# Hi and lo parts of the activations side by side: one 512-column matmul for the hi weights, sums added at eviction

## The chip, the cores and the metric

The kernel runs on one core of a Trainium2 chip. The metric is device microseconds of one execution; before the change the median of three runs is 1461.11 us.

## What is computed

Two layers of a decoder trunk on x of 256 tokens by 1,024 features, all in float32. Cut to what matters:

```python
for l in range(2):
    x = x + 0.5 * swiglu(rmsnorm(x, ffn1_norm[l]), ffn1_w_in[l], ffn1_w_out[l])
    h = rmsnorm(x, mix_norm[l])
    hq, hf, hi, hg, aq, ak, av, ga, gb = split(h @ w_in[l])
    A = hgrn2_recurrence(silu(hq), 1 - f, hi, log(f)); f = lb + (1 - lb) * sigmoid(hf)
    A = rms(A) * out_norm[l] * silu(hg)
    B = three groups of dilated window attention over aq, ak, av, merged
    x = x + (sigmoid(ga) * (A @ w_a[l]) + sigmoid(gb) * (B @ w_b[l])) @ w_out[l]
    x = x + 0.5 * swiglu(rmsnorm(x, ffn2_norm[l]), ffn2_w_in[l], ffn2_w_out[l])
# swiglu(h, w1, w2): a, b = split(h @ w1); (silu(a) * b) @ w2, inner width 2816
```

## The kernel before

**Three products for one.** TensorE multiplies in float32r, a shorter form of float32. To keep the precision, each operand is split into a hi part (rounded to float32r) and a lo part (the rest), and a product is the sum of three: hi weights with hi activations, hi weights with lo activations, lo weights with hi activations.

**Weights.** `unit` loads up to eight row tiles of 128 rows by 256 columns into a buffer `raw` (three of them). In chunks of four row tiles ScalarE copies them into `whi` (L195) and VectorE subtracts to give `wlo` (L196). There are four buffers of each, so two units of weights are held at a time.

**Two forms of product.** `mm_feat` (L209 to L211) keeps a 128 by 128 piece of weights in the array and streams 256 tokens of activations: the output has features in partitions and both blocks of 128 features (`fb`) lie side by side in one PSUM bank of 512 float32 columns. For each row tile and block it issues a triple: hi weights with `ah`, hi weights with `al`, lo weights with `ah`, all three added into the same 256 columns. `full` is `unit` and `mm_feat` over 1,024 rows: 48 matmuls. `wide` with `mm_half` (L219 to L221) does it the other way round: 128 tokens stay in the array and 512 weight columns stream, two banks for the two halves of the tokens. It serves where tokens are wanted in partitions (v, g, q, k, and the last product of the kernel).

**Activations.** `xh` and `xl` are the parts of the normed input (gains go in ahead of the product, and 1/rms comes in behind it through `Rb`, one factor per token, or `rstd`). `hh` and `hl` are the parts of the ffn's inner values, `oah` and `oal` (tile names `ph`, `pl`) those of the recurrence's output, `mgh` and `mgl` (the same tiles) those of the merged branches, `obh` and `obl` those of the attention's output. Each of these is a tile of its own: [128, k, 256].

**PSUM.** Eight banks: four (`MM`) in the pool `mm` for these products, one a `full`, two a `wide`; three `sm` and one `tr` for the small ones.

**Evictions.** A `full` is evicted by one VectorE instruction that reads the bank and multiplies by `Rb` (L307, L311, L352, L362, L660) or by another operand (L675, L684), or adds to `xT` (L342, L699).

**Stages of a layer.** `ffn` (22 units in, then three units for each of four output blocks), `mix` with the recurrence (`hgrn_pair`, four times), the gates A, the attention, the products with `w_a`, gates B mixed with `branch_b` (units of half the length), the product with `w_out`, then the second `ffn`. Behind each stage's start `norm_scale` makes `Rb` from the sum of squares, while the first units of the stage are already multiplied.

**Order.** Each engine runs its queue in order. The program is written stage by stage, but the framework lays out each engine's instructions itself with a simulated timeline (`schedule_with_timeline_sim`), so small products, evictions and splits of later units are mixed, and two units can be open at the same time. A tile of a pool that is used again waits until its last reader is done.

Of the kernel before, what the change touches and what calls it, by code (L numbers as in the profile page):

```python
# [37 lines left out]
# columns of the constant table  # L38
# [9 lines left out]
def _shape_constants():  # L48
    """Identity, rotary tables and 0/1 or additive masks: functions of the shapes alone."""
# [26 lines left out]
def trunk(ctx, tc, x, ffn1_norm, ffn1_w_in, ffn1_w_out, mix_norm, w_in, lb_logits, out_norm,  # L76
# [6 lines left out]
    ps_mm = ctx.enter_context(tc.tile_pool(name="ps_mm", bufs=MM, space=PSUM))  # L83
# [81 lines left out]
    def lower_bounds():  # L165
        """Lower bounds of the decay of layer 1: softmax over depth, cumulated, less the first."""
# [16 lines left out]
    def unit(w, r0, nk, col, step=0):  # L183
# [6 lines left out]
        for a in range(0, nk, step or KH):  # L190
            n = min(step or KH, nk - a)
            hi = wts.tile([128, KH, CU], F32R, name="whi", bufs=WB)
            lo = wts.tile([128, KH, CU], F32R, name="wlo", bufs=WB)
            r = raw[:, a:a + n, :]
            nc.scalar.activation(hi[:, :n, :], r, AF.Copy)  # L195
            nc.vector.tensor_sub(lo[:, :n, :], r, hi[:, :n, :].bitcast(F32))  # L196
            parts += [(hi[:, k, :], lo[:, k, :]) for k in range(n)]
        return parts

    def mm_feat(ps, wu, ah, al, k0, nk, first, last):  # L200
        """ps[feature, fb, token] += W^T a"""
        for k in range(nk):
            hi, lo = wu[k]
            for fb in range(2):
                o = ps[:, fb * T:(fb + 1) * T]
                f = slice(fb * 128, (fb + 1) * 128)
                s = first and k == 0 and fb == 0
                e = last and k == nk - 1
                nc.tensor.matmul(o, hi[:, f], ah[:, k0 + k, :], start=s, stop=False, skip_group_check=True)  # L209
                nc.tensor.matmul(o, hi[:, f], al[:, k0 + k, :], start=False, stop=False, skip_group_check=True)  # L210
                nc.tensor.matmul(o, lo[:, f], ah[:, k0 + k, :], start=False, stop=e, skip_group_check=True)  # L211

    def mm_half(o, h, wu, ah, al, k0, nk, first, last):
        """o[token of half h, column] += a^T W"""
# [8 lines left out]
    def full(w, col, ah, al, nk=KD, step=0):  # L223
        wu = unit(w, 0, nk, col, step)
        ps = ps_mm.tile([128, 512], F32, name="mm")
        mm_feat(ps, wu, ah, al, 0, nk, True, True)
        return ps

    def wide(w, col, ah, al, nk=KD):
# [18 lines left out]
    def v2(a):  # L248
        return a.rearrange("p (a b) -> p a b", a=2)

# [41 lines left out]
    def ffn(l, gi, w1, w2, to_out, x0=None):  # L292
        norm_parts(gi, l)
        with ExitStack() as es:
            fp = es.enter_context(tc.tile_pool(name="ffn", bufs=2))
            hh = fp.tile([128, KF, T], F32R, name="hh", bufs=1)
            hl = fp.tile([128, KF, T], F32R, name="hl", bufs=1)
            xt = None
            for j in range(DFF // CU):
                pa = full(w1, j * CU, xh, xl, step=0 if j or l or gi else FIRST)  # L300
# [6 lines left out]
                nc.vector.tensor_mul(a, v2(pa), Rb2)  # L307
                nc.scalar.activation(a, a, AF.Silu)
                pb = full(w1, DFF + j * CU, xh, xl)
                b = fp.tile([128, 2, T], F32, name="fb")  # L310
                nc.vector.tensor_mul(b, v2(pb), Rb2)  # L311
# [13 lines left out]
            if to_out:  # L325
                for c in range(D // CW):
                    ps = wide(w2, c * CW, hh, hl, KF)
# [5 lines left out]
            else:  # L333
                for c in range(D // CU):
                    ps = ps_mm.tile([128, 512], F32, name="mm")
                    k0 = 0
                    for nk in (8, 8, 6):
                        wu = unit(w2, k0 * 128, nk, c * CU)
                        mm_feat(ps, wu, hh, hl, k0, nk, k0 == 0, k0 + nk == KF)
                        k0 += nk  # L340
                    xs = xT[:, 2 * c:2 * c + 2, :]
                    nc.vector.scalar_tensor_tensor(xs, v2(ps), 0.5, xs, op0=OP.mult, op1=OP.add)  # L342

# [1 line left out]
    def hgrn_pair(wp, st, l, u, pf, vg):  # L345
        W, X, ATs = st
        w = w_in[l]
        if pf is None:
            pf = full(w, MIX_HF + u * CU, xh, xl)
        f = wp.tile([128, 2, T], F32, name="hf", bufs=2)  # L350
        k = wp.tile([128, 2, T], F32, name="hk", bufs=2)
        nc.vector.tensor_mul(f, v2(pf), Rb2)  # L352
# [6 lines left out]
        pq = full(w, MIX_HQ + u * CU, xh, xl)  # L359
        z = wp.tile([128, 2, T], F32, name="hz", bufs=1)  # L360
        sg = wp.tile([128, 2, T], F32, name="hs", bufs=1)
        nc.vector.tensor_mul(z, v2(pq), Rb2)  # L362
# [5 lines left out]
        if u % 2 == 0:  # L368
            pv = wide(w, MIX_HI + u * CU, xh, xl)
# [17 lines left out]
        def suffix(B, m, kin, name):  # L387
            """products behind each m-block inside its 4m-block, and the keys carried to its end"""
# [13 lines left out]
        def diag(Y, s0, m, dst):  # L402
            """queries decayed to the start of their 4m-block: slot j for the m-block j"""
# [48 lines left out]
        def carry(m, B, last=False):  # L452
            """queries and keys from blocks of m to blocks of 2m"""
# [37 lines left out]
        if u % 2:  # L491
            pg = wide(w, MIX_HG + (u - 1) * CU, xh, xl)
# [40 lines left out]
    def attn(ap, l, obh, obl):  # L533
# [5 lines left out]
        def qk_unit(i, base, dst, g):  # L539
# [6 lines left out]
            ps = wide(w, base + g * CW, xh, xl)  # L546
# [30 lines left out]
        def v_unit(g):  # L577
            ps = wide(w, MIX_AV + g * CW, xh, xl)
# [54 lines left out]
    def mix(l):  # L633
        norm_parts(1, l)
        with ExitStack() as es:
            mp = es.enter_context(tc.tile_pool(name="mix", bufs=1))
            pf0 = full(w_in[l], MIX_HF, xh, xl)
# [20 lines left out]
            def gate(base, u, dst):  # L658
                ps = full(w, base + u * CU, xh, xl)
                nc.vector.tensor_mul(dst, v2(ps), Rb2)  # L660
# [4 lines left out]
            with ExitStack() as e2:  # L665
                ap = e2.enter_context(tc.tile_pool(name="attn", bufs=1))
                obh = ap.tile([128, 4, T], F32R, name="obh")
                obl = ap.tile([128, 4, T], F32R, name="obl")
                attn(ap, l, obh, obl)
                if l == 0:  # L670
                    lower_bounds()
                for u in range(D // CU):
                    ps = full(w_a[l], u * CU, oah, oal)
                    s = slice(2 * u, 2 * u + 2)
                    nc.vector.tensor_mul(mg[:, s, :], mg[:, s, :], v2(ps))  # L675
                mgh = mp.tile([128, KD, T], F32R, name="ph", tag="ph", bufs=1)
                mgl = mp.tile([128, KD, T], F32R, name="pl", tag="pl", bufs=1)
                gb = {}

                def branch_b(u):  # L680
                    ps = full(w_b[l], u * CU, obh, obl, nk=4)
# [14 lines left out]
            for u in range(D // CU):  # L696
                ps = full(w_out[l], u * CU, mgh, mgl)
                xs = xT[:, 2 * u:2 * u + 2, :]
                nc.vector.tensor_add(xs, xs, v2(ps))  # L699
# [31 lines left out]
```

## Time and profile before

| | before |
|---|---|
| median of three runs | 1461.11 us (1460.61 to 1461.12) |
| span of the profiled execution | 1458.1 us |
| HBM read over the span | 250.39 MB, 172 GB/s |
| weight splits, ScalarE (L195, L241) | 367.9 + 132.6 us |
| weight splits, VectorE (L196, L242) | 424.2 + 155.2 us |
| matmuls and weight loads | 11,362 each |

The profile is of one execution. Its span runs from the first to the last instruction and is 3.0 us shorter than the median of the runs. PE is TensorE's matmuls, PEld its weight loads, DVE is VectorE, ACT is ScalarE, POOL is GpSimd. L209 is line 209 of the kernel. `mm<-xh,whi` means that tile `mm` is written from `xh` and `whi`. In a view of groups, "x1920 | 540.7, 282 | 1.4" are the count, the busy time in us, the mean of one in ns and the idle time before them. Matmuls overlap in the pipeline, so their busy times add up to more than the time that passes.

### The profile page before, as it was taken

How to read it: one execution, taken by the hardware profiler on the slowest of the kernel's cores; microseconds unless marked ns; L12 is line 12 of the kernel's file. 1: busy time of each engine (PE TensorE's matmuls, PEld its weight loads, DVE VectorE, ACT ScalarE, POOL GpSimd, SP SyncE). 2: the span in 40 equal slices, each digit the busy share in tenths (PEclk: the TensorE clock that was granted, in tenths of full speed). 3: DMA queues.
4: the chain of work that ended last, by engine and by line, in shares of the span. 5: the costliest groups of instructions: out<-in, count | busy, mean ns of one | idle time of the engine just before them, and what ended most of it. 6: DMA issues, size and time to landing. Idle time of an engine off the chain costs nothing.

```text
span 1458.1 us, 26998 instructions
## 1 busy us (share of the span) xinstructions
PE 1448.9 (99%) x11362; PEld 1366.3 (94%) x11362; DVE 996.0 (68%) x1452; ACT 791.1 (54%) x1259; POOL 91.3 (6%) x86
## 2 busy tenths in 40 slices
PE   8999999999999999999999999999999999999999
PEld 8999998898889999999999999988988899999987
DVE  6666559776976586665566655698779766766653
ACT  6544447667864555444444444566577646554432
POOL 0000010002510000000000000100034000000000
PEclk9999999999999999999999999999999999999999
DMA  9565564345554365555555555544454534555552
GB/s 309 176 195 177 178 203 156 135 145 174 173 174 146 115 202 176 196 178 186 190 174 190 186 164 189 197 147 144 149 173 171 179 125 138 195 186 191 174 187 101
DMA packets 215881, 253.17 MB, mean 174 GB/s; under 512 B 4224, under 2 KB 182608, under 8 KB 215760
## 3 DMA queue, kind: packets, MB, share of 16 engines
q1 hardware_dynamic: 215584, 251.38, 51.8%
q8 instruction: 89, 1.46, 0.4%
q14 instruction: 32, 0.26, 0.1%
q10 hardware_dynamic: 176, 0.07, 0.0%
HBM read 250.39 MB, written 1.05 MB: 172 GB/s over the span
## 4 chain that ended last, share of the span: by engine, by line
PE 99%; DMA 0%; ACT 0%; SPq 0%; DVE 0%; issue 0%; ACTq 0%
PE mm L209 23%; PE mm L211 23%; PE mm L210 23%; PE mm L221 8%; PE mm L219 8%; PE mm L220 8%; PE sm L415 1%; PE sm L595 1%; PE tr L574 1%; PE sm L614 1%; PE sm L606 1%; PE sm L616 0%; DMA x<-in_x_dram 0%; PE sm L480 0%; PE sm L525 0%; PE sm L506 0%
## 5 line engine op out<-in xcount | busy, mean ns | idle before, releaser
L195 ACT ACTIVATE whi<-raw 128x1024 fp32r<-128x1024 f32 (+1 forms) x354 | 367.9, 1041 | 435.4 <-PE mm L210 339.8
L196 DVE TENSOR_TENSOR wlo<-raw,whi 128x1024 fp32r<-128x1024 f32 (+1 forms) x354 | 424.2, 1199 | 244.3 <-ACT whi L195 242.6
L209 PE MATMUL mm<-xh,whi 128*128 128x256 f32 x1920 | 540.7, 282 | 1.4 <-ACT whi L195 1.4
L211 PE MATMUL mm<-xh,wlo 128*128 128x256 f32 x1920 | 540.9, 282 | 0.0
L210 PE MATMUL mm<-xl,whi 128*128 128x256 f32 x1920 | 539.4, 281 | 0.0
L209 PEld LDWEIGHTS mm<-xh,whi 128*128 128x128 f32 x1920 | 362.6, 189 | 2.8 <-ACT whi L195 1.8
L211 PEld LDWEIGHTS mm<-xh,wlo 128*128 128x128 f32 x1920 | 362.5, 189 | 1.2 <-issue 0.4
L210 PEld LDWEIGHTS mm<-xl,whi 128*128 128x128 f32 x1920 | 362.4, 189 | 0.6
L242 DVE TENSOR_TENSOR wlo<-raw,whi 128x1024 fp32r<-128x1024 f32 x126 | 155.2, 1233 | 62.5 <-ACT whi L241 62.2
L241 ACT ACTIVATE whi<-raw 128x1024 fp32r<-128x1024 f32 x126 | 132.6, 1060 | 98.0 <-PE mm L221 53.1
L219 PE MATMUL mm<-whi,xh 128*128 128x512 f32 x416 | 166.7, 401 | 0.0
L221 PE MATMUL mm<-whi,xl 128*128 128x512 f32 x416 | 165.8, 399 | 0.0
L220 PE MATMUL mm<-wlo,xh 128*128 128x512 f32 x416 | 164.8, 396 | 0.0
L211 PE MATMUL mm<-hh,wlo 128*128 128x256 f32 x528 | 149.5, 283 | 0.0
L210 PE MATMUL mm<-hl,whi 128*128 128x256 f32 x528 | 149.5, 283 | 0.0
L209 PE MATMUL mm<-hh,whi 128*128 128x256 f32 x528 | 149.4, 283 | 0.0
L210 PEld LDWEIGHTS mm<-hl,whi 128*128 128x128 f32 x528 | 100.8, 191 | 0.0
L211 PEld LDWEIGHTS mm<-hh,wlo 128*128 128x128 f32 x528 | 100.8, 191 | 0.0
L209 PEld LDWEIGHTS mm<-hh,whi 128*128 128x128 f32 x528 | 100.8, 191 | 0.0
L221 PEld LDWEIGHTS mm<-whi,xl 128*128 128x128 f32 x416 | 78.1, 188 | 18.4
L220 PEld LDWEIGHTS mm<-wlo,xh 128*128 128x128 f32 x416 | 78.2, 188 | 17.7
L219 PEld LDWEIGHTS mm<-whi,xh 128*128 128x128 f32 x416 | 78.2, 188 | 16.9
(194 smaller groups left out, 1753.2 us busy)
## 6 DMA issues: line engine op xcount, KB each, us to landing
raw<-in_ffn_w_in_dram SPq DMA_DIRECT2D x87, 1024.0 KB, 5.1
raw<-in_w_in_dram SPq DMA_DIRECT2D x84, 1024.0 KB, 4.9
raw<-in_ffn_w_out_dram SPq DMA_DIRECT2D x34, 1024.0 KB, 5.1
raw<-in_ffn_w_out_dram SPq DMA_DIRECT2D x12, 768.0 KB, 4.4
raw<-in_w_branch_a_dram SPq DMA_DIRECT2D x8, 1024.0 KB, 5.1
raw<-in_w_out_dram SPq DMA_DIRECT2D x8, 1024.0 KB, 5.4
raw<-in_w_branch_b_dram SPq DMA_DIRECT2D x8, 512.0 KB, 3.4
x<-in_x_dram SPq DMA_DIRECT2D x4, 256.0 KB, 4.0
```

The source lines that it names most:

```text
L195: nc.scalar.activation(hi[:, :n, :], r, AF.Copy)
L196: nc.vector.tensor_sub(lo[:, :n, :], r, hi[:, :n, :].bitcast(F32))
L209: nc.tensor.matmul(o, hi[:, f], ah[:, k0 + k, :], start=s, stop=False, skip_group_check=True)
L210: nc.tensor.matmul(o, hi[:, f], al[:, k0 + k, :], start=False, stop=False, skip_group_check=True)
L211: nc.tensor.matmul(o, lo[:, f], ah[:, k0 + k, :], start=False, stop=e, skip_group_check=True)
L219: nc.tensor.matmul(o, ah[:, k0 + k, t], hi, start=s, stop=False, skip_group_check=True)
L220: nc.tensor.matmul(o, ah[:, k0 + k, t], lo, start=False, stop=False, skip_group_check=True)
L221: nc.tensor.matmul(o, al[:, k0 + k, t], hi, start=False, stop=e, skip_group_check=True)
L241: nc.scalar.activation(hi, r, AF.Copy)
L242: nc.vector.tensor_sub(lo, r, hi.bitcast(F32))
L415: nc.tensor.matmul(p[32 * b:32 * b + 32, c * n:(c + 1) * n], kk[:, o], mov(o), start=True, stop=True, tile_position=(0, 32 * b))
L574: nc.tensor.transpose(pt[:, h, c * 128:(c + 1) * 128], z[:, c, 2 * a + h, :], ident)
```

## The change

The two parts of every activation go into one tile, side by side for each row tile: `xp` is [128, k, 2, 256], with `xh` and `xl` as views of it, and `hp`, `oap`, `mgp` and `obp` likewise. In `mm_feat` the hi weights are loaded once and stream both parts as 512 columns into a whole bank, so the products with hi and with lo activations lie in its two halves; the lo weights stream the hi part into the second half. Each block of 128 features has a bank of its own, so a unit takes two banks, and the pool has two tiles of two banks in place of four of one. The sum of the halves is made at eviction: `total` copies the second halves with ScalarE and adds the first halves with VectorE, and what multiplied from PSUM then multiplies in SBUF. Where the result is added to `xT`, two VectorE instructions add the halves one after the other. Some tiles get 32 more columns, and their data starts a few columns later. Comments are dropped.

```diff
-    ps_mm = ctx.enter_context(tc.tile_pool(name="ps_mm", bufs=MM, space=PSUM))
+    ps_mm = ctx.enter_context(tc.tile_pool(name="ps_mm", bufs=MM // 2, space=PSUM))
...
+    def parts_of(pool, n, name, at, tag=None):
+        t = pool.tile([128, n * 2 * T + 32], F32R, name=name, tag=tag or name, bufs=1)
+        return t[:, at // 4:at // 4 + n * 2 * T].rearrange("p (k a t) -> p k a t", a=2, t=T)
...
-    xh = const.tile([128, KD, T], F32R, name="xh")
-    xl = const.tile([128, KD, T], F32R, name="xl")
+    xp = const.tile([128, KD, 2, T], F32R, name="xp")
+    xh, xl = xp[:, :, 0, :], xp[:, :, 1, :]
...
-            hi = wts.tile([128, KH, CU], F32R, name="whi", bufs=WB)
-            lo = wts.tile([128, KH, CU], F32R, name="wlo", bufs=WB)
+            hi, lo = (wts.tile([128, KH * CU + 32], F32R, name=x, bufs=WB)[:, 0:KH * CU].rearrange(
+                "p (k c) -> p k c", c=CU) for x in ("whi", "wlo"))
...
-                o = ps[:, fb * T:(fb + 1) * T]
                 f = slice(fb * 128, (fb + 1) * 128)
-                s = first and k == 0 and fb == 0
                 e = last and k == nk - 1
-                nc.tensor.matmul(o, hi[:, f], ah[:, k0 + k, :], start=s, stop=False, skip_group_check=True)
-                nc.tensor.matmul(o, hi[:, f], al[:, k0 + k, :], start=False, stop=False, skip_group_check=True)
-                nc.tensor.matmul(o, lo[:, f], ah[:, k0 + k, :], start=False, stop=e, skip_group_check=True)
+                nc.tensor.matmul(ps[:, fb, :], hi[:, f], ap[:, k0 + k].rearrange("p a t -> p (a t)"),
+                                 start=first and k == 0, stop=False, skip_group_check=True)
+                nc.tensor.matmul(ps[:, fb, T:2 * T], lo[:, f], ap[:, k0 + k, 0, :], start=False, stop=e,
+                                 skip_group_check=True)
...
+    def banks():
+        return ps_mm.tile([128, 2, 512], F32, name="mm")
...
+    def total(dst, ps):
+        nc.scalar.activation(dst, ps[:, :, T:2 * T], AF.Copy)
+        nc.vector.tensor_add(dst, ps[:, :, 0:T], dst)
...
     def wide(...)
-        ps = [ps_mm.tile([128, 512], F32, name="mm") for _ in range(2)]
+        pt = banks()
+        ps = [pt[:, h, :] for h in range(2)]
...
-                hi = wts.tile([128, KH, CU], F32R, name="whi", bufs=WB).rearrange("p (k a) c -> p k (a c)", a=2)
-                lo = wts.tile([128, KH, CU], F32R, name="wlo", bufs=WB).rearrange("p (k a) c -> p k (a c)", a=2)
+                hi, lo = (wts.tile([128, KH * CU + 32], F32R, name=x, bufs=WB)[:, 8:8 + KH * CU].rearrange(
+                    "p (k c) -> p k c", c=CW) for x in ("whi", "wlo"))
...
     def ffn(...)
-            hh = fp.tile([128, KF, T], F32R, name="hh", bufs=1)
-            hl = fp.tile([128, KF, T], F32R, name="hl", bufs=1)
+            hp = parts_of(fp, KF, "hp", 64)
+            hh, hl = hp[:, :, 0, :], hp[:, :, 1, :]
...
-                nc.vector.tensor_mul(a, v2(pa), Rb2)
+                total(a, pa)
+                nc.vector.tensor_mul(a, a, Rb2)
...
-                    nc.vector.scalar_tensor_tensor(xs, v2(ps), 0.5, xs, op0=OP.mult, op1=OP.add)
+                    for a in range(2):
+                        nc.vector.scalar_tensor_tensor(xs, ps[:, :, a * T:(a + 1) * T], 0.5, xs,
+                                                       op0=OP.mult, op1=OP.add)
...
     def hgrn_pair(...)
-        nc.vector.tensor_mul(f, v2(pf), Rb2)
+        total(f, pf)
+        nc.vector.tensor_mul(f, f, Rb2)
...
     def mix(l)
-            oah = mp.tile([128, KD, T], F32R, name="ph", tag="ph", bufs=1)
-            oal = mp.tile([128, KD, T], F32R, name="pl", tag="pl", bufs=1)
+            oap = parts_of(mp, KD, "pp", 96)
+            oah, oal = oap[:, :, 0, :], oap[:, :, 1, :]
+            et = mp.tile([128, 2, T], F32, name="et", bufs=1)
...
-                obh = ap.tile([128, 4, T], F32R, name="obh")
-                obl = ap.tile([128, 4, T], F32R, name="obl")
+                obp = parts_of(ap, 4, "obp", 0)
...
-                    nc.vector.tensor_mul(mg[:, s, :], mg[:, s, :], v2(ps))
+                    total(et, ps)
+                    nc.vector.tensor_mul(mg[:, s, :], mg[:, s, :], et)
...
                 def branch_b(u)
-                    nc.vector.tensor_mul(g, g, v2(ps))
+                    total(et, ps)
+                    nc.vector.tensor_mul(g, g, et)
...
-                nc.vector.tensor_add(xs, xs, v2(ps))
+                for a in range(2):
+                    nc.vector.tensor_add(xs, xs, ps[:, :, a * T:(a + 1) * T])
```

The other units (`pb`, `pq`, the gates) change as `pa` and `pf` do.

More of the change, by code (lines that the diff above doesn't have):

```diff
@@ L198, in unit, with mm_feat @@
         return parts
-    def mm_feat(ps, wu, ah, al, k0, nk, first, last):
+    def mm_feat(ps, wu, ap, k0, nk, first, last):
         for k in range(nk):
@@ L221, in mm_half, with full, wide @@
             nc.tensor.matmul(o, al[:, k0 + k, t], hi, start=False, stop=e, skip_group_check=True)
-    def full(w, col, ah, al, nk=KD, step=0):
+    def banks():
+        return ps_mm.tile([128, 2, 512], F32, name="mm")
+    def full(w, col, ap, nk=KD, step=0):
         wu = unit(w, 0, nk, col, step)
-        ps = ps_mm.tile([128, 512], F32, name="mm")
-        mm_feat(ps, wu, ah, al, 0, nk, True, True)
-        return ps
-    def wide(w, col, ah, al, nk=KD):
-        ps = [ps_mm.tile([128, 512], F32, name="mm") for _ in range(2)]
+        ps = banks()
+        mm_feat(ps, wu, ap, 0, nk, True, True)
+        return ps
+    def total(dst, ps):
+        nc.scalar.activation(dst, ps[:, :, T:2 * T], AF.Copy)
+        nc.vector.tensor_add(dst, ps[:, :, 0:T], dst)
+    def wide(w, col, ap, nk=KD):
+        pt = banks()
+        ps = [pt[:, h, :] for h in range(2)]
+        ah, al = ap[:, :, 0, :], ap[:, :, 1, :]
         for k0 in range(0, nk, 4):
@@ L306, in ffn @@
                 a = fp.tile([128, 2, T], F32, name="fa")
-                nc.vector.tensor_mul(a, v2(pa), Rb2)
+                total(a, pa)
+                nc.vector.tensor_mul(a, a, Rb2)
                 nc.scalar.activation(a, a, AF.Silu)
-                pb = full(w1, DFF + j * CU, xh, xl)
+                pb = full(w1, DFF + j * CU, xp)
                 b = fp.tile([128, 2, T], F32, name="fb")
-                nc.vector.tensor_mul(b, v2(pb), Rb2)
+                total(b, pb)
+                nc.vector.tensor_mul(b, b, Rb2)
                 nc.vector.tensor_mul(a, a, b)
@@ L326, in ffn @@
                 for c in range(D // CW):
-                    ps = wide(w2, c * CW, hh, hl, KF)
+                    ps = wide(w2, c * CW, hp, KF)
                     for h in range(2):
@@ L334, in ffn @@
                 for c in range(D // CU):
-                    ps = ps_mm.tile([128, 512], F32, name="mm")
+                    ps = banks()
                     k0 = 0
@@ L358, in hgrn_pair @@
         nc.scalar.activation(k, f, AF.Copy, scale=-1.0, bias=1.0)
-        pq = full(w, MIX_HQ + u * CU, xh, xl)
+        pq = full(w, MIX_HQ + u * CU, xp)
         z = wp.tile([128, 2, T], F32, name="hz", bufs=1)
         sg = wp.tile([128, 2, T], F32, name="hs", bufs=1)
-        nc.vector.tensor_mul(z, v2(pq), Rb2)
+        total(z, pq)
+        nc.vector.tensor_mul(z, z, Rb2)
         nc.scalar.activation(sg, z, AF.Sigmoid)
@@ L368, in hgrn_pair @@
         if u % 2 == 0:
-            pv = wide(w, MIX_HI + u * CU, xh, xl)
+            pv = wide(w, MIX_HI + u * CU, xp)
             vg["v"] = wp.tile([128, 2, CW], F32, name="hv", bufs=1)
@@ L491, in hgrn_pair @@
         if u % 2:
-            pg = wide(w, MIX_HG + (u - 1) * CU, xh, xl)
+            pg = wide(w, MIX_HG + (u - 1) * CU, xp)
             vg["g"] = wp.tile([128, 2, CW], F32, name="hgs", bufs=1)
@@ L545, in qk_unit @@
             nc.gpsimd.tensor_mul(gs[:, :, 64:128], sin_t[:, :, 64:128], gr[:, None, 0:64].to_broadcast([128, 2, 64]))
-            ps = wide(w, base + g * CW, xh, xl)
+            ps = wide(w, base + g * CW, xp)
             z = ap.tile([128, 2, 4, 128], F32, name="az", bufs=2)
@@ L577, in v_unit @@
         def v_unit(g):
-            ps = wide(w, MIX_AV + g * CW, xh, xl)
+            ps = wide(w, MIX_AV + g * CW, xp)
             for c in range(2):
@@ L658, in gate @@
             def gate(base, u, dst):
-                ps = full(w, base + u * CU, xh, xl)
-                nc.vector.tensor_mul(dst, v2(ps), Rb2)
+                ps = full(w, base + u * CU, xp)
+                total(dst, ps)
+                nc.vector.tensor_mul(dst, dst, Rb2)
                 nc.scalar.activation(dst, dst, AF.Sigmoid)
@@ L666, in mix @@
                 ap = e2.enter_context(tc.tile_pool(name="attn", bufs=1))
-                obh = ap.tile([128, 4, T], F32R, name="obh")
-                obl = ap.tile([128, 4, T], F32R, name="obl")
-                attn(ap, l, obh, obl)
+                obp = parts_of(ap, 4, "obp", 0)
+                attn(ap, l, obp[:, :, 0, :], obp[:, :, 1, :])
                 if l == 0:
```

18 lines of the change are left out of this document (9 added, 9 removed).

## The prediction

> **What bounds the kernel now.** I read the page's busy times first, then the clock, then the chain that ended last.
>
> ```profile
> span 1458.1 us, 26998 instructions
> PE 1448.9 (99%) x11362; PEld 1366.3 (94%) x11362; DVE 996.0 (68%) x1452; ACT 791.1 (54%) x1259; POOL 91.3 (6%) x86
> ...
> PEclk9999999999999999999999999999999999999999
> ...
> PE 99%; DMA 0%; ACT 0%; SPq 0%; DVE 0%; issue 0%; ACTq 0%
> ```
>
> TensorE works in 99% of the span at a granted clock of 0.9 or more in every slice, and 99% of the chain lies on it. VectorE and ScalarE have 32% and 46% of the span free. So the time is the sum of the distances from one matmul's start to the next (the pitch), and other work counts only where it makes TensorE wait. A busy record (282 ns for 256 columns) overlaps the next one and is no price; the pitch is. I take it from the view of one source line over a stretch without other matmuls: count, first start, last start.
>
> ```profile
> L209 PE MATMUL mm<-xh,whi x285: 277/280/387, 29.7 to 129.8; 128*128 128x256 f32 x143
> L209 PE MATMUL mm<-xh,whi x293: 277/281/285, 555.8 to 660.0; 128*128 128x256 f32 x147
> L209 PE MATMUL mm<-hh,whi x173: 277/283/283, 136.8 to 198.8; 128*128 128x256 f32 x173
> L209 PE MATMUL mm<-ph,whi x56: 283/283/283, 521.0 to 540.8; 128*128 128x256 f32 x56
> L219 PE MATMUL mm<-whi,xh x33: 392/399/399, 338.1 to 360.5; 128*128 128x512 f32 x33
> L219 PE MATMUL mm<-whi,hh x79: 389/389/397, 1396.0 to 1449.5; 128*128 128x512 f32 x79
> ```
>
> L209 runs once in a triple (L209, L210, L211). A triple of 256 columns takes 100.1/284 = 352.5 ns and 104.2/292 = 356.8 ns on xh, 62.0/172 = 360.5 on hh, 19.8/55 = 360.0 on ph: 117.5 to 120.2 ns a matmul. In `wide`, L219 to L221 take 22.4/32 = 700 ns with xh and 53.5/78 = 686 with hh: 233.3 and 228.6 ns for 512 columns. So 512 columns cost 1.90 to 1.99 times what 256 cost. The whole change lives in that gap.
>
> **The matmuls.** How many triples there are, by the grouped view:
>
> ```profile
> L209 PE MATMUL mm<-xh,whi 128*128 128x256 f32 x1920 | 540.7, 282 | 1.4 <-ACT whi L195 1.4
> L209 PE MATMUL mm<-hh,whi 128*128 128x256 f32 x528 | 149.4, 283 | 0.0
> L209 PE MATMUL mm<-ph,whi 128*128 128x256 f32 x256 | 71.6, 283 | 0.0
> L209 PE MATMUL mm<-obh,whi 128*128 128x256 f32 x64 | 18.2, 285 | 0.0
> L219 PE MATMUL mm<-whi,xh 128*128 128x512 f32 x416 | 166.7, 401 | 0.0
> L219 PE MATMUL mm<-whi,hh 128*128 128x512 f32 x88 | 34.3, 390 | 0.0
> ```
>
> Each of the 2,768 triples becomes a pair: one matmul of 512 columns with the hi weights, one of 256 with the lo weights. Streamed columns stay at 768; one matmul and one weight load go. Triples now: 1,920 x 354.7 (mean of the two xh rows) + 528 x 360.5 + 320 x 360.0 = 986.5 us, 356.4 each. After: no row shows the pair alternating. I take 512 at 228.6 and 256 at 356.4/3 = 118.8, so 347.4 a pair, 961.6 us: **24.9 us less**. Ends by rows: 228.6 + 117.5 = 346.1 saves 28.5 us; 233.3 + 120.2 = 353.5 saves 8.0. A loss is excluded, since even this dearest pair is below the mean triple. Far below lies the score product, which streams 256 float32 columns of both parts in 1.30/6 = 216.7 ns:
>
> ```profile
> 442.52 1.30 PE sm L595 x6
> ```
>
> A pair at 216.7 + 117.5 = 334.2 would save 61.4 us. I stay with 228.6 because it is the row with the same type, columns and weight loads.
>
> A rule speaks against the change: the Trainium skill, page "TensorE: Matmul & The Clock Gate", section "Back-to-back issue gap", gives 262 cycles at 2.4 GHz for 256 columns and 518 for 512. By it (an estimate) a triple is 327.5 ns and a pair 325.0, so the edit would save 6.9 us instead of 24.9. The trace disagrees in size: 117.5 to 120.2 and 228.6 to 233.3 ns stand against the rule's 109.2 and 215.8.
>
> **The wide matmuls** keep shape and count but their operands move. In the program before, xh starts at byte 24,704 of a partition, whi at 83,168, hh at 124,128: remainders by 128 of 0, 96 and 96. The faster wide row has equal remainders (whi with hh), the slower one unequal. The diff starts `wide`'s weights 32 bytes later, so they meet xp at 0 and 0 and hp (64 bytes later) at 0 and 32. If that is what parts the rows, 3 x 416 matmuls gain 4.7 ns and 3 x 88 lose it: **4.7 us less**. Two rows are thin ground; the ends are 0 and 5.9, and I take 4.7.
>
> **The evictions.** `total` adds, for 136 units, a ScalarE copy of 512 elements from PSUM and a VectorE add; the 20 units that end in xT get a second VectorE instruction. Nearest rows:
>
> ```profile
> L307 DVE TENSOR_TENSOR fa<-mm,Rb 128x512 f32<-128x512 f32 x44 | 30.4, 691 | 21.1 <-PE mm L211 21.0
> L580 ACT ACTIVATE av<-mm,rstd 128x512 f32<-128x512 f32 x12 | 8.2, 685 | 10.2 <-PE mm L221 10.2
> L342 DVE SCALAR_TENSOR_TENSOR xT<-mm,xT 128x512 f32<-128x512 f32 x12 | 8.2, 684 | 0.0
> ```
>
> ScalarE gets 136 x 0.685 = 93 us (884 of some 1,440), VectorE 156 x 0.69 = 108 (1,104). Neither becomes the bound; the copies lie under matmuls. What can show is latency. The add waits for the copy, with the splits (wlo) of the next units queued behind it on VectorE, and TensorE waits for those. And a unit now holds two banks: with four banks, unit n+2 may start only when unit n is evicted (before: unit n+4). In the ffn a unit lasts 16 x 347.4 = 5.6 us and its eviction some 0.7 + 0.7 plus up to one queued split of 1.2, so nothing shows. Three places are tighter:
>
> ```profile
> 200.00:260.00 60.00, 60.00 (x595) 53.81 (x594) 50.57 (x98) 39.44 (x63) 5.62 (x5) 1.00 0.52 174
> 510.00:530.00 20.00, 20.00 (x169) 20.00 (x168) 17.30 (x21) 10.22 (x13) 0.00 (x0) 1.00 0.64 211
> 1453.14 0.69 DVE L330 SCALAR_TENSOR_TENSOR fy<-mm,xt 128x512 f32<-128x512 f32 x1 [7.20 <-PE mm L221]
> 1454.49 0.69 DVE L330 SCALAR_TENSOR_TENSOR fy<-mm,xt 128x512 f32<-128x512 f32 x1 [0.67 <-PE mm L221]
> ```
>
> Columns after the stretch: PE, PEld, DVE, ACT busy. In the first pairs of `hgrn_pair` VectorE works 50.6 of 60 us and gets 4 adds (2.8); in `branch_b` 17.3 of 20 and gets 5 (3.5), while units of 24 matmuls become 2.8 us long and turn banks over twice as fast. I put 2 us to each, twice (two layers), and 1 us to stage borders and to the end, where both halves of the last product now share one tile (an eviction of 0.69 us may move behind the last matmul): **9 us more**, between 2 (all hidden) and 40 (the slower rival below).
>
> **The sum**, against the profiled execution: 1458.1 - 24.9 - 4.7 + 9 = 1437.5. Its span is 3.0 us below the median of the runs, 1461.1; with that, **1440.5 us**.
>
> **Rivals.**
>
> *The excess goes by columns, not by matmuls* (0.20). For: on xh, 233.3 is nearly 2 x 117.5. Against: on hh, 228.6 against 240.4. Then a pair is 353.5 and the wide rows stay: 1461.1 - 8.0 + 9 = 1462, spread 1455 to 1468. This is the side on which the skill's rule for the back-to-back gap falls, too.
>
> *Slower: half the banks stall TensorE at each norm* (0.13). The first units behind a norm are evicted late today, because the eviction multiplies by Rb:
>
> ```profile
> 211.92 0.40 PE L219 MATMUL mm<-whi,xh 128*128 128x512 f32 x1
> ...
> 218.24 0.69 DVE L352 TENSOR_TENSOR hf<-mm,Rb 128x512 f32<-128x512 f32 x1
> ...
> 552.32 1.23 DVE L196 TENSOR_TENSOR wlo<-raw,whi 128x1024 fp32r<-128x1024 f32 x1 [2.72 <-ACT whi L195]
> ...
> 555.79 0.28 PE L209 MATMUL mm<-xh,whi 128*128 128x256 f32 x1
> ...
> 558.56 0.69 DVE L307 TENSOR_TENSOR fa<-mm,Rb 128x512 f32<-128x512 f32 x1
> ```
>
> The third unit starts at 211.92 and the first is free at 218.93: 7.0 us short in each of two mixers. In three ffns it is 559.25 - 555.79 = 3.5. Together 24.4 us, and 5 x 1.38 for the longer eviction: 31, and with the other 9 some 40, against 29.6 gained: 1471. It decides if the add stands behind the copy into Rb on VectorE, as the code's order has it. Against it: the new pair of instructions doesn't read Rb, VectorE is idle for 2.72 us ahead of 552.32 when the first unit is done, and its order there (splits between the norm's steps) is already not the code's.
>
> *Much faster: the weight load paces the short matmuls, and a 512-column stream runs free* (0.12). A pair at 334.2 gives 1461.1 - 61.4 + 9 = 1409. Against: both wide rows have one load to 512 columns and still take 228.6 or more. By the skill's same page, section "LDWEIGHTS (loading the stationary operand)", 128 columns take 106.7 ns, as long as 256 columns take to stream, which is the case for this rival; the PEld share of 94% fits it.
>
> **Chances.** Forecast 0.55, with its own range 1426 to 1456. Within 0.2% (2.9 us, about what a measurement of this kernel can tell from no change) lies half of the by-columns rival and a little of the slower one: 0.11. Faster: 0.55 + 0.12 + 0.05 = 0.72. Slower: 0.17. The range 1415 to 1466 takes in the forecast, most of the by-columns rival and the near edges of the other two.
>
> **What would show it.** PE at 8,594 matmuls, down by 2,768. The pitch of a pair in the ffn: 346 to 349 right, near 353 the by-columns rival, near 334 the fast one. `wide` on xp at 228 to 229 a matmul. Waits of PE for VectorE or ScalarE behind a norm below 1 us each; 3 to 7 there is the slower rival. VectorE near 1,104 us and ScalarE near 884. I am wrong if a 512-column matmul next to a 256-column one costs what neither costs among its own kind, or if the order in which the program is laid out pulls the evictions to another place.

## The result and the profile after

The changed kernel takes 1521.18 us (median of 4 runs, 1518.87 to 1521.86), the kernel before 1461.11: the ratio is 1.041, with an interval of 1.0398 to 1.0423. The forecast was 1440.5 us and faster; the range ended at 1466. Both the sign and the size were wrong.

The page of the changed kernel, with the lines that were read first before the change:

```profile
span 1518.9 us, 21864 instructions
...
PE 1450.7 (96%) x8594; PEld 1241.0 (82%) x8594; DVE 1087.0 (72%) x1608; ACT 861.4 (57%) x1399; POOL 88.3 (6%) x86
...
PEclk9999999999999999999999999999989999999999
...
PE 90%; DVE 4%; ACT 3%; POOL 1%; issue 1%; DMA 0%; POOLq 0%; SPq 0%; DVEq 0%; ACTq 0%
```

The matmuls are down to 8,594, as they should be, and neither VectorE nor ScalarE comes near its bound. But the span is 60.8 us longer, and TensorE is busy for 1.8 us more, so its idle time grew by 59.0 us, from 9.2 to 68.2. It also ran slower for a part: the mean granted clock fell from 1.000 to 0.983. By the trace's clock records, ten stretches of 3.4, 6.8 or 10.2 us, 51.2 us in all, are at half clock (an eleventh begins at 1517.0, behind the last matmul). TensorE works in 41.0 us of them. If half clock doubles a matmul's time, that work would take 20.5 us at full clock. So the balance is +59.0 of waiting, +20.5 of half clock, and -18.7 of matmul work (the rest of 60.8).

Where it went is read from the view of windows, one window for each stage (first ffn, mixer, second ffn, for each layer; the borders are the first and last matmuls of the stages). Columns are the stretch, its length, then PE, PEld, DVE, ACT and POOL busy, the clock, the DMA share and GB/s. Before:

```profile
9.90:200.10 190.20, 190.19 (x1587) 189.77 (x1588) 119.25 (x143) 95.29 (x111) 0.70 (x1) 1.00 0.62 203
200.10:543.90 343.80, 343.80 (x2620) 309.01 (x2619) 263.07 (x457) 216.09 (x424) 42.74 (x39) 1.00 0.48 160
543.90:733.20 189.30, 189.30 (x1593) 189.30 (x1592) 116.59 (x131) 89.87 (x103) 1.71 (x1) 1.00 0.56 183
733.20:922.40 189.20, 189.20 (x1593) 189.20 (x1592) 116.08 (x129) 87.08 (x99) 1.71 (x1) 1.00 0.56 184
922.40:1266.60 344.20, 344.20 (x2620) 308.84 (x2619) 264.25 (x465) 215.41 (x424) 42.46 (x39) 1.00 0.48 160
1266.60:1454.10 187.50, 187.50 (x1345) 177.10 (x1343) 112.71 (x122) 82.16 (x89) 1.72 (x1) 1.00 0.51 170
```

After:

```profile
10.70:197.90 187.20, 187.18 (x1058) 163.68 (x1059) 132.17 (x169) 105.44 (x133) 0.70 (x1) 1.00 0.63 205
197.90:574.50 376.60, 349.89 (x2204) 294.34 (x2203) 280.81 (x483) 230.07 (x450) 41.61 (x39) 0.97 0.45 147
574.50:761.10 186.60, 185.24 (x1063) 162.42 (x1062) 131.30 (x159) 100.18 (x125) 1.53 (x1) 1.00 0.56 184
761.10:947.70 186.60, 185.22 (x1063) 162.46 (x1062) 130.26 (x155) 97.29 (x121) 1.53 (x1) 1.00 0.57 186
947.70:1327.20 379.50, 352.39 (x2205) 295.42 (x2204) 282.96 (x491) 230.36 (x450) 41.06 (x39) 0.96 0.45 146
1327.20:1514.20 187.00, 186.20 (x989) 159.50 (x988) 124.97 (x146) 92.86 (x111) 1.62 (x1) 1.00 0.52 169
```

All four ffns got shorter, by 3.0, 2.7, 2.6 and 0.5 us, 8.8 together. The two mixers got longer by 32.8 and 35.3. TensorE idles 26.7 and 27.1 us in them, where before it didn't idle at all, and only there the clock is below 1.00. The view of waits, TensorE's alone, names what it waited for (total, times, longest):

```profile
PE mm L223 <- ACT az L581: 25.4, 6, 7.0
PE sm L626 <- DVE as L622: 8.7, 2, 4.4
PE mm L212 <- DVE et L239: 8.5, 6, 2.9
PE tr L300 <- POOL rstd L297: 7.5, 5, 2.0
...
PE mm L223 <- DVE hf L239: 2.2, 2, 1.1
```

Before, that view has no such line: TensorE waited for the first loads, and once for a split. L223 is the first matmul of a `wide` unit and `az` (L581) the eviction of a q or k product: the largest item is not one of the evictions that the change lengthened. It is a product that keeps its shape and its eviction, but whose two banks are now one tile. The timelines of the first mixer show it, TensorE's first (start, duration, line, operation):

```profile
359.74 0.39 PE L225 MATMUL mm<-whi,xp 128*128 128x512 f32 x1
367.13 0.80 PE L223 MATMUL mm<-whi,xp 128*128 128x512 f32 x1 [7.00 <-ACT az L581]
367.72 0.63 PE L224 MATMUL mm<-wlo,xp 128*128 128x512 f32 x1
368.15 0.63 PE L225 MATMUL mm<-whi,xp 128*128 128x512 f32 x1
...
370.44 0.39 PE L225 MATMUL mm<-whi,xp 128*128 128x512 f32 x1
```

and ScalarE's:

```profile
361.13 1.13 ACT L581 ACTIVATE az<-mm,ass 128x128 f32<-128x128 f32 x4
362.13 0.38 ACT L573 ACTIVATE asq<-mm,rstd 128x128 f32<-128x128 f32 x1
...
365.94 1.13 ACT L581 ACTIVATE az<-mm,ass 128x128 f32<-128x128 f32 x4
```

The same two evictions of a product before the change:

```profile
353.73 1.13 ACT L561 ACTIVATE az<-mm,ass 128x128 f32<-128x128 f32 x4
...
356.09 1.12 ACT L561 ACTIVATE az<-mm,ass 128x128 f32<-128x128 f32 x4
```

At 359.74 TensorE finishes its second q or k product and both tiles of the pool are full. ScalarE evicts the first half of one from 361.13 to 362.26 (four records of 128 columns), and then squares eight more blocks of 128 columns until 366. The second half goes at 365.94 and ends at 367.07; TensorE starts at 367.13. Before, each half was a tile, and two things differ. A bank was freed by itself; that alone would help little here, because a product's first six matmuls (about 1.4 us) fill its first bank and the next six the second. And ScalarE's queue was laid out otherwise: both halves were squared first, and the second was evicted soon behind the first. From the end of one eviction to the end of the other it is 1.3 to 4.7 us in all kernels with single banks (before, e3, e5 to e7, e9, e11) and 4.8 to 8.4 us in all with joined tiles (the changed kernel, e1, e2, e4, e8). Why the framework orders them so isn't shown. The 7.0 us are followed by a second loss: the distance between starts is 0.43 us at 367.72 and some 0.23 from 370.44 on, that is half clock until about 370.

The other place is `branch_b`. VectorE's rows there:

```profile
536.32 1.22 DVE L201 TENSOR_TENSOR wlo<-raw,whi 128x1024 fp32r<-128x1024 f32 x1 [2.03 <-ACT whi L200]
537.47 0.68 DVE L239 TENSOR_TENSOR et<-mm,et 128x512 f32<-128x512 f32 x1
```

and TensorE's next unit:

```profile
538.20 0.80 PE L212 MATMUL mm<-obp,whi 128*128 128x512 f32 x1 [2.89 <-DVE et L239]
```

The add that frees the banks stands behind a split of the next weights, though the copy that it needs (L238 on ScalarE) ended at 536.78. TensorE starts at 538.20, after 2.89 us of waiting for this `et`. The other open unit, one of the gates B, finished before 523 and is evicted only from 541.02 on, so TensorE had no bank to go on with.

### The profile page after: what moved, and what is told of

Read it like the earlier page. It is cut to its first block, busy times and chain, and to the rows that moved or that the text cites. A ratio compares the mean times of both kernels' runs of the same rounds, so it can differ in the third digit from the quotient of the medians.

```text
span 1518.9 us, 21864 instructions
## 1 busy us (share of the span) xinstructions
PE 1450.7 (96%) x8594; PEld 1241.0 (82%) x8594; DVE 1087.0 (72%) x1608; ACT 861.4 (57%) x1399; POOL 88.3 (6%) x86
## 3 DMA queue, kind: packets, MB, share of 16 engines
q1 hardware_dynamic: 215584, 251.38, 50.6%
## 4 chain that ended last, share of the span: by engine, by line
PE 90%; DVE 4%; ACT 3%; POOL 1%; issue 1%; DMA 0%; POOLq 0%; SPq 0%; DVEq 0%; ACTq 0%
PE mm L212 41%; PE mm L214 21%; PE mm L223 7%; PE mm L225 7%; PE mm L224 7%; PE sm L435 1%; DVE wlo L256 1%; PE sm L615 1%; DVE wlo L201 1%; PE sm L634 1%; ACT az L581 1%; ACT asq L573 1%; ACT whi L200 1%; ACT whi L255 1%; PE sm L626 1%
## 5 line engine op out<-in xcount | busy, mean ns | idle before, releaser
L212 PE MATMUL mm<-xp,whi 128*128 128x512 f32 x1920 | 674.4, 394 | 5.2 <-DVE gb L239 2.7
L214 PE MATMUL mm<-xp,wlo 128*128 128x256 f32 x1920 | 541.0, 282 | 0.0
L212 PEld LDWEIGHTS mm<-xp,whi 128*128 128x128 f32 x1920 | 361.2, 188 | 84.8 <-DVE gb L239 3.3
L214 PEld LDWEIGHTS mm<-xp,wlo 128*128 128x128 f32 x1920 | 362.5, 189 | 1.3 <-DVE wlo L201 0.4
L223 PE MATMUL mm<-whi,xp 128*128 128x512 f32 x416 | 170.0, 409 | 27.7 <-ACT az L581 25.4
L212 PE MATMUL mm<-hp,whi 128*128 128x512 f32 x528 | 186.5, 396 | 0.0
L225 PE MATMUL mm<-whi,xp 128*128 128x512 f32 x416 | 168.5, 405 | 0.0
L224 PE MATMUL mm<-wlo,xp 128*128 128x512 f32 x416 | 168.3, 405 | 0.0
L214 PE MATMUL mm<-hp,wlo 128*128 128x256 f32 x528 | 148.6, 282 | 0.0
L223 PEld LDWEIGHTS mm<-whi,xp 128*128 128x128 f32 x416 | 80.9, 194 | 47.1 <-ACT az L581 27.1
L212 PEld LDWEIGHTS mm<-hp,whi 128*128 128x128 f32 x528 | 99.3, 188 | 24.0
L225 PEld LDWEIGHTS mm<-whi,xp 128*128 128x128 f32 x416 | 80.5, 193 | 17.9
```

Source lines behind the costliest of these rows:

```text
L212: nc.tensor.matmul(ps[:, fb, :], hi[:, f], ap[:, k0 + k].rearrange("p a t -> p (a t)"), start=first and k == 0, stop=False, skip_group_che ...
L214: nc.tensor.matmul(ps[:, fb, T:2 * T], lo[:, f], ap[:, k0 + k, 0, :], start=False, stop=e, skip_group_check=True)
L223: nc.tensor.matmul(o, ah[:, k0 + k, t], hi, start=s, stop=False, skip_group_check=True)
L224: nc.tensor.matmul(o, ah[:, k0 + k, t], lo, start=False, stop=False, skip_group_check=True)
L225: nc.tensor.matmul(o, al[:, k0 + k, t], hi, start=False, stop=e, skip_group_check=True)
```

## The experiments

After the result stood four theories. **BANKS**: with two open units in place of four, and two banks freed at once, TensorE runs out of banks wherever evictions bunch. Its rival, **EVICTION**: the work that the evictions add to ScalarE and VectorE makes them late. **REMAINDER**: part of the pitch is set by where operands start in their partition (by 128 bytes). **ET**: the single tile for the sum in the mixer holds the evictions up. Others came with the runs.

### Half the banks without the pairs (e1)

The kernel before, with the new pool; a `full` uses one bank of its tile.

```diff
-    ps_mm = ctx.enter_context(tc.tile_pool(name="ps_mm", bufs=MM, space=PSUM))
+    ps_mm = ctx.enter_context(tc.tile_pool(name="ps_mm", bufs=MM // 2, space=PSUM))
...
+    def banks():
+        return ps_mm.tile([128, 2, 512], F32, name="mm")
...
-        ps = ps_mm.tile([128, 512], F32, name="mm")
+        ps = banks()[:, 0, :]
...
-        ps = [ps_mm.tile([128, 512], F32, name="mm") for _ in range(2)]
+        pt = banks()
+        ps = [pt[:, h, :] for h in range(2)]
```

> The kernel before with one edit: the pool of the big products holds two tiles of two banks, and a unit of 48 matmuls takes a whole tile though it fills one bank of it. Triples, evictions and data layout stay. Theory BANKS (half as many units in flight make TensorE wait, and the waits cost it the clock): TensorE idle 45 us or more above before, stretches at half clock, 1500 to 1550 us. Theory EVICTION (the copy and the add per unit, their time and their wait for each other, make TensorE wait): 1458 to 1466 us, no half clock.

1507.23 us, ratio 1.0314 (1.0294 to 1.0335): 46 us slower with not one matmul or eviction changed. Its waits of TensorE:

```profile
PE mm L219 <- ACT az L565: 19.9, 7, 4.3
```

Four banks in two joined tiles, with the order that the framework lays out for them, make the wait for `az` without any pair. A `wide` product took two banks before, too, so for q and k it is the joining and not the number. The clock falls to 0.993. The time is where BANKS had it, but TensorE's idle time grew by 34.0 us (to 43.2) and not by the 45 expected.

### The changed kernel with one read an eviction (e2)

```diff
-        total(a, pa)
-        nc.vector.tensor_mul(a, a, Rb2)
+        nc.vector.tensor_mul(a, pa[:, :, 0:T], Rb2)
```

and so at every `total`; at the additions to `xT` only the first of the two instructions stays. The second halves are left out of the sums.

> The changed kernel with the eviction of before: one instruction that reads the first halves of the two banks; the second halves (products with a lo part) are left out of the sum. Pairs and the pool of two tiles of two banks stay. BANKS: 1500 to 1525 us, the waits in the mixers stay. EVICTION: 1430 to 1445 us, TensorE idle as before the change.

1488.53 us, ratio 1.0186 (1.0166 to 1.0207): 33 us less than the changed kernel, yet 28 slower than before. It lies between the two theories; neither carries the loss alone. The wait for `az` stays, those for `et` and `as` are gone:

```profile
PE mm L223 <- ACT az L576: 19.7, 8, 5.5
```

The comparison isn't clean: here an eviction reads `Rb` again, as before the change, and behind the norms TensorE waits 5.9 us for `fa` and 4.0 for `hf`.

### The same remainder for every operand (e4)

```diff
-            hp = parts_of(fp, KF, "hp", 64)
+            hp = parts_of(fp, KF, "hp", 32)
...
-            oap = parts_of(mp, KD, "pp", 96)
+            oap = parts_of(mp, KD, "pp", 32)
...
-                obp = parts_of(ap, 4, "obp", 0)
+                obp = parts_of(ap, 4, "obp", 32)
```

(`mgp` as `oap`.) All of these then stand to the weights as `xp` does.

> The changed kernel with hp, pp and obp moved so that they start at the remainder by 128 bytes that xp has. Theory REMAINDER (where the operands start sets the pitch): the pair on hp goes from 353 ns to 347 to 349, on pp from 351 to 347 to 349, and the last product's 512-column matmuls from 233.5 to 227 to 229; the time falls by some 5 us to 1516. If the start doesn't matter: pitches as in the changed kernel.

1513.99 us (one run), 7.2 below the changed kernel; the spans, 1512.2 and 1518.9, are 6.7 apart. The view of one source line gives the pitch of a pair in the ffn's second product, first for the changed kernel, where its first product stands beside it:

```profile
L212 PE MATMUL mm<-xp,whi x284: 390/391/396, 29.6 to 128.0; 128*128 128x512 f32 x142
L212 PE MATMUL mm<-hp,whi x172: 388/397/400, 136.6 to 197.0; 128*128 128x512 f32 x172
L223 PE MATMUL mm<-whi,hp x88: 388/395/398, 1452.8 to 1513.7; 128*128 128x512 f32 x88
```

and then for e4:

```profile
L212 PE MATMUL mm<-hp,whi x171: 389/391/397, 136.9 to 195.9; 128*128 128x512 f32 x171
```

60.4/171 = 353.2 ns become 59.0/170 = 347.1, as on xp (98.4/283 = 347.7). So the start of hp matters, as REMAINDER had it, and it is 7 us of the 60 (e8, which has the same starts, is at 1514.06). One part was missed: the last product's 512-column matmuls went from 233.3 to 60.0/261 = 229.9 ns, where 227 to 229 was expected. The waits stay as they were (26.4 us for `az`, 8.7 for `as`, 8.6 for `et`).

### A second tile for the sum (e8)

e4, with every other unit's sum in the storage of `azs`:

```diff
+                def e_(u):
+                    return ap.tile([128, 2, 2, 128], F32, name="azs", bufs=1).rearrange(
+                        "p a b c -> p a (b c)") if u % 2 else et0
...
+                    et = e_(u)
                     total(et, ps)
```

> As e4, with a second tile for the sum of the halves: the products with w_a and w_b use et in turn with a tile that the attention no longer needs. Theory ET (branch_b is slow because each unit's sum waits until the last one is multiplied): the stretch of branch_b falls from 38 us a layer to 25, 1485 to 1500 us. Theory LOAD (copy, add and split simply fill ScalarE and VectorE there): within 4 us of e4's 1514.

1514.06 us, the same as e4; the waits for the sum are 5.8 for `et` and 3.3 for `azs` in place of 8.6. ET falls: the sum's tile isn't what the adds wait for. The time is LOAD's.

### Pairs in the ffns only (e3, e5)

e3 keeps triples and four single banks in the mixers, so each stage opens a pool of its own, two joined tiles in an ffn and four banks in a mixer:

```diff
+            pool["two"] = es.enter_context(tc.tile_pool(name="ps_mm", bufs=MM // 2, space=PSUM))
...
+            pool["one"] = es.enter_context(tc.tile_pool(name="ps_mm", bufs=MM, space=PSUM))
...
-            pf = full(w, MIX_HF + u * CU, xp)
+            pf = trip(w, MIX_HF + u * CU, xp)
```

> Pairs, two tiles of two banks and the longer eviction in the four ffns alone; in the mixers the triples, four single banks and the single-instruction eviction of before, on the same activation tiles. Both theories put the loss in the mixers and the gain of the ffns at some 9 us (their stretches in the two traces): 1448 to 1456 us. If the gain of the ffns is lost at the borders between the pools: 1458 to 1466.

1458.83 us, ratio 0.9987 (0.9977 to 0.9996): the gain expected was missed. TensorE's waits:

```profile
PE mm L241 <- DVE xT L385: 6.6, 2, 3.3
...
PE mm L212 <- DVE xT L385: 3.3, 1, 3.3
```

At three borders the next stage's first unit waits 3.3 us for the last eviction of the pool before it, and half clock follows. Within the ffns the joined tiles make no wait. That gave a new theory, **BORDER**: the change of pools makes these waits; against it, that the longer eviction at the end of a stage does. e5 has one pool of four single banks for everything; a pair's unit takes two of them and frees each by itself:

```diff
+    def banks():
+        return [ps_mm.tile([128, 512], F32, name="mm") for _ in range(2)]
...
+    def total(dst, ps):
+        for b in range(2):
+            nc.scalar.activation(dst[:, b, :], ps[b][:, T:2 * T], AF.Copy)
+            nc.vector.tensor_add(dst[:, b, :], ps[b][:, 0:T], dst[:, b, :])
```

and the remainders of e4.

> As e3 (pairs in the ffns, triples in the mixers), but all from one pool of four single banks: a pair takes two of them, each evicted by itself, so no pool ends between the stages; and hp, pp, obp start at the remainder of xp. Theory BORDER (the three waits of 3.6 us and the half clock behind them in e3 come from the change of pools): they go, and with 5 us from the remainders 1438 to 1450 us. If they come from the longer eviction at the stage's end: 1450 to 1458.

1438.48 us, ratio 0.9846 (0.9832 to 0.9859): faster than both kernels. From its page and its view of one source line:

```profile
span 1435.9 us, 23629 instructions
...
PE 1426.8 (99%) x9426; PEld 1266.3 (88%) x9426; DVE 1065.7 (74%) x1664; ACT 839.5 (58%) x1435; POOL 93.2 (6%) x86
```

```profile
L212 PE MATMUL mm<-hp,whi x170: 390/391/396, 136.8 to 195.5; 128*128 128x512 f32 x170
L212 PE MATMUL mm<-xp,whi x283: 390/391/396, 29.8 to 127.8; 128*128 128x512 f32 x142
```

The waits of e3 are gone, the clock is 1.000, a pair takes 58.7/169 = 347.3 and 98.0/282 = 347.5 ns. The time is BORDER's; but e5 also frees each bank by itself, and the two were not parted.

### How much of that is the layout (e7)

The kernel before with triples and its four banks, but with the operands at the remainders of e4:

```diff
-            hh = fp.tile([128, KF, T], F32R, name="hh", bufs=1)
+            hh = moved(fp, KF, "hh")
```

(`moved` makes a tile that is 32 columns longer, with the data from byte 32 on; likewise `hl`, `ph`, `pl`, `obh`, `obl` and the weights of `wide`.)

> The kernel before, triples and all, with hh, hl, ph, pl, obh, obl 32 bytes later and the weights of wide 32 bytes later, so that streamed operands stand to the kept ones as xh to whi did. REMAINDER: triples on hh and ph from 360 ns to 352 to 356, 512-column matmuls on xh from 233 to 227 to 231: 1447 to 1453 us, and the pair's own share of e5 is what e5 gains beyond that. If the start doesn't matter: 1459 to 1462.

1448.63 us, ratio 0.9914 (0.9901 to 0.9928): 12.7 us less with nothing but starts of tiles moved.

```profile
L212 PE MATMUL mm<-xh,whi x284: 277/280/392, 30.3 to 129.8; 128*128 128x256 f32 x142
L212 PE MATMUL mm<-hh,whi x175: 280/280/283, 137.2 to 199.0; 128*128 128x256 f32 x175
L212 PE MATMUL mm<-xh,whi x300: 277/280/367, 549.7 to 655.0; 128*128 128x256 f32 x150
L222 PE MATMUL mm<-whi,hh x76: 389/393/404, 1390.1 to 1442.4; 128*128 128x512 f32 x76
```

A triple takes 99.5/283 = 351.6 ns on xh and 61.8/174 = 355.2 on hh (before 354.7 and 360.5). For the ffns' 1,408 triples on xh and 528 on hh the pair's own gain in e5 is then 1,408 x (351.6 - 347.5) + 528 x (355.2 - 347.3) = 9.9 us; the times of e7 and e5 differ by 10.2.

The forecast of the time came true, but two rows don't follow the remainders. On xh in the second ffn a triple takes 105.3/299 = 352.2 ns, where it took 356.8, though neither xh nor these weights changed their remainder. In `wide` on hh both operands moved by the same 32 bytes, so their remainders stay equal, and a matmul went from 228.6 to 52.3/225 = 232.4 ns. So starts matter, but the remainder by 128 is not the whole rule.

### Pairs everywhere, with single banks (e6)

e4 with the `banks` and the `total` of e5. Theory **JOINED**: it is the release of two banks at once that costs most, not their number.

> As e4 (pairs everywhere, same remainders; 1514 us), but four single banks in place of two tiles of two: each bank is released by itself, and the eviction is made per bank (two copies and two adds of 256 columns). Theory JOINED (a product of q or k waits because both banks of a tile are released together): the waits of 3 to 7 us among the q and k products go, 1485 to 1500 us. Theory IN FLIGHT (two units at a time are too few, however they are released) or EVICTION LOAD: 1505 to 1530.

1469.77 us, ratio 1.0059 (1.0041 to 1.0078): 44 us less than e4, more than expected. What is left of TensorE's waits:

```profile
PE mm L212 <- DVE et L240: 7.9, 8, 1.5
PE mm L223 <- ACT az L582: 6.4, 1, 6.4
...
PE sm L627 <- DVE as L623: 4.4, 2, 4.2
PE tr L300 <- POOL rstd L297: 3.9, 2, 2.0
```

The wait for `az` fell from 26.4 to 6.4. Single banks take most of it away, as JOINED had it. But e6 also evicts each bank of a pair by itself, in halves of 256 columns, and the order on ScalarE changed with the tiles: a product's second half is evicted 1.3 to 4.7 us behind the first, in e4 4.8 to 8.4. The three were not parted. Still, e6 is 31 us above e5, all of the mixers' doing.

### What is left in the mixers (e9, e11)

e9 is e6 with one VectorE instruction a bank that reads the first half only; the second halves are left out of the sums.

```diff
-        total(f, pf)
-        nc.vector.tensor_mul(f, f, Rb2)
+        for b in range(2):
+            nc.vector.tensor_mul(f[:, b, :], pf[b][:, 0:T], Rb2[:, b, :])
```

> The kernel of e6 (pairs everywhere, four single banks, remainders equal), but each bank is evicted by one VectorE instruction that reads only its first half; the products in the second halves are left out of the sum, so ScalarE's copies and VectorE's adds are gone. e6 stands at 1469.8 us, the kernel with pairs in the ffns alone (e5) at 1438.5. If the rest between the two (31 us) is the work and the latency of the longer eviction in the mixers (theory EVICTION): 1432 to 1442, no wait of TensorE for VectorE or ScalarE over 1.5 us except the two behind the norm. If it is that only two units can be open at once, whatever an eviction costs (theory IN FLIGHT): 1458 to 1470, the waits of L212 for et and of L223 for az stay at their size. If both carry it: 1445 to 1455.

1459.84 us, ratio 0.9989 (0.998 to 0.9999). The time is IN FLIGHT's, but not its rows: the waits for `et` and `az` are gone, and others stand there.

```profile
PE sm L621 <- DVE as L617: 5.7, 2, 2.9
PE mm L212 <- DVE fa L238: 5.1, 3, 2.9
...
PE mm L223 <- DVE hf L238: 4.0, 2, 2.1
```

`hf` and `fa` are the first units behind a norm. In e9 their eviction multiplies by `Rb` again and must wait for it; with room for two units TensorE waits with it. So e9 took one cause away (it is 10 us faster than e6) and brought another in, and doesn't part the two cleanly.

e11 is e5 with pairs also in the gates A, the product with `w_a` and the product with `w_out`; the recurrence, the gates B and `branch_b` keep triples.

```diff
-                    ps = trip(w_a[l], u * CU, oap)
-                    nc.vector.tensor_mul(mg[:, s, :], mg[:, s, :], v2(ps))
+                    ps = full(w_a[l], u * CU, oap)
+                    total(et, ps)
+                    nc.vector.tensor_mul(mg[:, s, :], mg[:, s, :], et)
```

> The kernel of e5 with pairs (two single banks, eviction per bank) also in three places of the mixer whose neighbours are other units of full length: the gates A, the product with w_a, the product with w_out; the recurrence, the gates B and branch_b keep triples. 384 more triples become pairs, at 354.9 to 347.4 ns: 2.9 us less. If the loss in the mixers lies in the recurrence and in branch_b alone (theory PLACES): 1434 to 1437, no new wait over 1 us. If a unit of two banks costs anywhere that other work shares VectorE (theory ANYWHERE): 1441 to 1450, waits of TensorE at L212 behind the last attention units, and a clock below 1.000.

1437.75 us, ratio 0.984 (0.9824 to 0.9857), clock 1.000, and no new wait above 0.5 us. This is 0.7 us below e5, within the spread of both, where 1434 to 1437 was expected. So pairs do no harm in these three places, and bring next to nothing. By exclusion what e6 loses to e5 is brought in by the pairs of the recurrence, the gates B and `branch_b`: short units, and units among chains of small products. That they need more than two units open is argued, not shown, and which of them costs how much was not tried.

## Why the prediction was wrong

**Number of matmuls: right.** 8,594.

**The pair: right on xp.** 347.4 ns were forecast and 347.7 measured, and not by luck: the distance of starts is 229.7 ns behind a 512-column matmul and 117.9 behind one of 256, where 228.6 and 118.8 were put in; the by-columns rival (353.5) and the fast one (334.2) fall. The Trainium skill's rule for the gap (page "TensorE: Matmul & The Clock Gate", section "Back-to-back issue gap") had given 325.0, and the measurement decides against it. On hp it is 353.2, because the diff starts hp at a remainder 32 bytes beyond xp's. The prediction used the remainder for `wide` alone and not for pairs; that is the 7 us that e4 takes back. Two of its rows were not quite free of other matmuls (two small transposes in 555.8 to 660.0, four in 1396.0 to 1449.5), which changes their pitch by less than 1%.

**What the 24.9 us were made of: mis-assigned.** The prediction set triples of 356.4 against pairs of 347.4 and put the whole difference down to the pair. e7 shows triples at 351.6 and 355.2 with moved operands alone. With these (the second for ph and obh, too) the triples would take 976.3 us. So of the 24.9 us some 10 are the starts of the tiles and some 15 the pair (an estimate).

**The wide matmuls: direction right.** On hp they went from 228.6 to 60.9/261 = 233.3 ns, as forecast. On xp the distance of neighbouring starts averages 230.7 (233.4 before), not 228.6: half of the gain. Altogether TensorE's work fell by 18.7 us (its busy time, less the half clock) where 29.6 were forecast.

**The evictions, "9 us more": the step that failed.** Their work was sized well: VectorE 1,087 us (1,104 forecast), ScalarE 861 (884). "Neither becomes the bound" was right and beside the point. What it cost is 59.0 us of idle TensorE and 20.5 of half clock, some 80 in place of 9. Two things were missed. First, the "three places" were the recurrence's first pairs, `branch_b` and the kernel's end. The attention's q and k products weren't among them; their shape and eviction stayed. Yet their two banks became one tile: the prediction saw that for the last product ("both halves of the last product now share one tile") and priced it only there. It was the largest item of waiting, 25.4 us in six times. e1 shows it without any pair, and in e6 it falls to 6.4 with single banks. Second, the prediction looked at busy shares (50.6 of 60 us, 17.3 of 20), not at who would stand behind whom. The add in `branch_b` stands behind a split of 1.22 us, and both open units were waiting for their eviction, so TensorE stood still. The prediction's warning, that the order laid out might move the evictions, came true at the softmax: TensorE waits 4.4 us there for `as`, in each layer, where before other units lay.

**The slower rival: right in kind, wrong in place.** It named half the banks, and put the stall at the norms with 7.0 us in each mixer. There it is 1.96 + 1.11 us, and some 10 over all five norms. The stall of 7.0 us came at the q and k products instead. The forecast's range ended at 1466, short even of this rival's own 1471, although the trace of before had no row against the mechanism elsewhere.

**The clock: not in the sum at all.** Half clock behind the waits took about a third as much as the waits.

## What to carry to other kernels

When a change halves the number of open accumulators, list every user of the pool, those that it doesn't touch too, and ask of each how long after its last matmul the last reader ends, and whether banks are freed one by one or together. Look again at the order of each engine's queue, which can change with the tiles. A tile of two banks is freed by the later of two readers: keep banks as tiles of their own, and use the costly form only where the work beside it is even (here the ffns: 0.9846 with pairs there, of which the starts of the tiles alone give 0.9914; 1.041 with pairs everywhere in joined tiles). Before a gain in pitch is put down to an instruction's shape, measure the old shape with its operands at the new addresses.

## What the runs showed of the hardware

**Starts of operands.** Moving tiles by 32 bytes changed the pitch of float32r matmuls by 1 to 2% (a pair on hp from 353.2 to 347.1 ns in e4, a triple on hh from 360.5 to 355.2 in e7), and the kernel by 12.7 us (e7). Why isn't shown. The starts by 128 bytes forecast most of it, but two rows of e7 go against them.

**Short waits cost the clock.** The windows around the mixer's norm in the changed kernel:

```profile
206.00:213.00 7.00, 4.09 (x26) 3.41 (x24) 4.53 (x6) 3.52 (x6) 2.91 (x2) 1.00 0.45 150
213.10:216.50 3.40, 3.34 (x8) 2.66 (x9) 3.27 (x8) 3.04 (x6) 3.40 (x4) 0.50 0.89 304
216.50:220.00 3.50, 3.50 (x17) 2.84 (x16) 3.50 (x11) 2.07 (x5) 0.03 (x1) 1.00 0.01 4
```

TensorE waited 1.96 us and, after two transposes, 1.11 us. Then 8 matmuls start in 3.40 us, where behind them 17 start in 3.50: the clock is 0.50 for 3.4 us. The Trainium skill, page "TensorE: Matmul & The Clock Gate", section "What's actually happening", has half rate after at least one idle window of about 3.4 us and full rate after one busy window, the windows running freely. The stretches agree with that, all up to the last matmul being 3.4, 6.8 or 10.2 us, and in each trace they start whole multiples of 3.413 us apart. But a window need not be idle throughout. Take the windows of this grid at full clock in the eight traces that have half clock before their last matmul (without their first 10 us). All with less than 1.45 us of busy TensorE were followed by half clock (49 of 49), and none with more than 1.66 us (0 of 3,326); between these, 4 of 13 were. By that, one wait of some 2 us (3.41 - 1.45) can be enough if it falls into a single window. Here the window before 213.1 held nearly all of both waits and, but for the two transposes, no matmul.
